# Latent attention: exponentials divided before they are transposed, feature-major output, and output weights split early through DRAM

## The chip, the cores and the metric

The kernel runs on one core of a Trainium2 chip. The metric is device time in microseconds (us), lower is better. The core has five instruction streams: TensorE (PE: matmuls and transposes, with its weight loads, PEld, beside them), VectorE (DVE), ScalarE (ACT), GpSimd (POOL) and SyncE (SP, which here only issues DMA loads). Each stream runs its instructions in order; they wait for one another by semaphores. DMAs are issued by SP, by ACT (stores) or by POOL.

## What is computed

One layer of an encoder for two sequences, a prompt of 256 tokens and a sample of 1024, with the same weights, in fp32. Cut to what the change touches:

```python
h = rmsnorm(x, attn_norm_g); proj = h @ w_in
a = mla_group(...)        # latent attention, 8 heads of 64: softmax(q k^T) v
b = na_group(...)         # neighbourhood attention on a grid, 8 heads of 64
mix = concatenate([rmsnorm(a, mla_out_g), rmsnorm(b, na_out_g)])   # 512 + 512
x = x + mix @ w_o                                                  # 1024 x 1024
h2 = rmsnorm(x, ffn_norm_g)
x = x + (silu(h2 @ w_gate) * (h2 @ w_up)) @ w_down
```

The norm of each half of `mix` is one number per token and half; the gains are folded into the rows of `w_o`.

## The kernel before

The 1280 tokens are ten tiles of 128. To keep fp32 accuracy, operands are split in a high and a low part, and a product is three matmuls, `mm3` (L108 to L112): high by high, high by low, low by high. The stages follow one another on PE, by the time of the profile:

- 0 to 138 us: the first norm, the latents, the rotary keys, the first neighbourhood projections.
- 138 to 193: the values of the neighbourhood attention (L383 to L397). The eight 128x512 blocks of `w_v` are loaded into `wv_raw` slots (eight buffers) and split into `wv_h` on ACT (L134) and `wv_l` on DVE (L135). Then each token tile is 24 matmuls into a PSUM tile `na_t` (two buffers), which ACT copies to `V` (L397).
- 193 to 380: the neighbourhood attention in four pairs of heads. For each pair SP loads tables of bias (`mi_s` and `mp_s` once, then `g_s` and `g_p`), and POOL adds them up to `b_s` (L434) and `b_p` (L449). POOL also splits the weights of the next pair's queries and keys, `wqk_raw` to `wqk_h` and `wqk_l` (L331, L94, L96), and copies queries into zeroed tiles `qz` (L411, L485). The projections of the next pair (`pj`) run on PE between the heads' work.
- 380 to 669: the latent attention, `attend` (L743 to L809). The unit of work is one head `i` of a pair and one chunk of 256 queries, done in two halves `u` of 128. For a half of the sample there are six score matmuls of 128x512 into `S` (128x1024), the negated maximum on DVE (L770), the exponential with its sum `l` on ACT (L772) into `ex` (two buffers), eight PE transposes of 128x128 into `tp` (L778), and their split to `PT`, a copy on ACT (L99) and a subtraction on DVE (L100). After both halves come 16 matmuls `o` (L788), which give a transposed output with the high and the low values' parts in the two halves of its 128 rows. ACT copies it to `os` (L792), PE transposes it back (two of L796), ACT copies it to `ob` (L798), DVE takes reciprocals of the sums (`mr`, L800), POOL adds the two parts (L801) and multiplies by the reciprocal (L805), and ACT's queue stores `at` token-major to `a_d`.
- 660 to 791: output projection, norm and the FFN's input, tile by tile. `mix_in` (L863) loads a token tile's two halves from `a_d` and `b_d`, ACT sums squares (L873), POOL works out the two factors (`rstd_of`) and scales both halves (L877). `mix_T` transposes them (eight `trm`, L888) and splits them to `mT`. `out_proj` (L897) does 24 matmuls for each half of the columns in one PSUM bank `po`, and DVE adds the residual (L907). The output weights are loaded raw before that by SP, and POOL multiplies them by the gain (L855) and splits them (L94, L96), 24 operations in all, between 597 and 639 us.
- 791 to 1610: the FFN.

SP's loads are issued in the order of the program text (`manual_schedule`). The order of the other streams is made by a scheduler from dependences and its own costs. A tile pool of n buffers makes the writer of buffer use k wait for the readers of use k - n, and memory that one pool gives up is handed to later pools, whose first writers then wait for the last users of it.

## Time and profile before

| what | us |
|---|---|
| median of three runs (1612.18 to 1613.88) | 1613.79 |
| span of the profiled execution | 1610.3 |
| PE busy | 1582.5 |
| DVE busy | 893.3 |
| ACT busy | 717.2 |
| POOL busy | 666.1 |

The profiled execution's own time lies within the three runs; its span, from the first instruction to the last, is 3.5 us under the median. In the views a row is a line of the kernel, an engine, an operation and `out<-in`, with a count; then the total busy time and the mean time of one in ns, and the idle time of the engine ahead of it with what ended that. In a timeline row the first number is the start and the second the length. Matmuls overlap: each row's length is longer than the distance to the next. PE's granted clock is 0.99 to 1.00 in all stages.

### The profile page before, as it was taken

Reading aid. Unit: us, or ns where it says so; the run is one execution under the profiler, and the core shown is the slowest. Engines: PE = TensorE matmul, PEld = TensorE weight load, DVE = VectorE, ACT = ScalarE, POOL = GpSimd, SP = SyncE. Lnnn points to the kernel's source line nnn. Section 1 sums busy time; section 2 is a strip of 40 time slices with the busy share of each in tenths; the row PEclk is TensorE's granted clock in tenths of the full one; section 3 lists DMA queues with packets and bytes.
Section 4 is the critical chain, followed back from the end, with each engine's and each line's share of the span. In section 5 each row is a group of like instructions: output and inputs, shape, how many; then the busy total and the mean of one; then the engine's idle time right before and its main releaser. Section 6 shows DMA issues by size and latency. Waiting matters only on the chain.

```text
span 1610.3 us, 25767 instructions
## 1 busy us (share of the span) xinstructions
PE 1582.5 (98%) x9616; PEld 1443.1 (90%) x9616; DVE 893.3 (55%) x1501; ACT 717.2 (45%) x1492; POOL 666.1 (41%) x833
## 2 busy tenths in 40 slices
PE   8999999999999999999999999999999999999998
PEld 8998789998888888888899999999999998888886
DVE  5853045566677777443583444334444246886676
ACT  6533144465777777544453323233222332443334
POOL 4633235544211129224676665565666651010002
PEclk9999999999999999999999999999999999999999
DMA  8626022152100030234312232222232237843534
GB/s 294 202 70 160 19 53 63 37 209 62 32 20 26 24 119 20 80 118 144 125 67 65 89 110 97 71 87 89 97 110 76 70 128 269 296 140 96 157 103 155
DMA packets 121772, 171.09 MB, mean 106 GB/s; under 512 B 35376, under 2 KB 65840, under 8 KB 121648
## 3 DMA queue, kind: packets, MB, share of 16 engines
q1 hardware_dynamic: 78880, 120.30, 24.3%
q10 hardware_dynamic: 41952, 46.08, 8.2%
q0 software_dynamic: 816, 3.08, 0.5%
q8 instruction: 75, 1.23, 0.3%
q14 instruction: 49, 0.40, 0.1%
HBM read 118.96 MB, written 50.46 MB: 105 GB/s over the span
## 4 chain that ended last, share of the span: by engine, by line
PE 90%; POOL 3%; ACT 2%; DVE 2%; DMA 1%; issue 1%; SPq 0%; ACTq 0%; POOLq 0%; DVEq 0%
PE M L112 11%; PE M L110 10%; PE M L111 10%; PE d L111 5%; PE d L110 5%; PE d L112 5%; PE o L788 4%; PE tp L778 4%; PE na_o L512 3%; PE po L110 2%; PE pj L110 2%; PE pj L111 2%; PE pj L112 2%; PE po L111 2%; PE po L112 2%; PE S L110 2%
## 5 line engine op out<-in xcount | busy, mean ns | idle before, releaser
L111 PE MATMUL M<-S,wc 128*128 128x320 f32 x1056 | 323.8, 308 | 0.0
L110 PE MATMUL M<-S,wc 128*128 128x320 f32 x1056 | 321.3, 309 | 2.5 <-ACT S L962 1.2
L112 PE MATMUL M<-S,wc 128*128 128x320 f32 x1056 | 312.0, 309 | 2.4 <-POOL wc L970 2.4
L110 PEld LDWEIGHTS M<-S,wc 128*128 128x128 f32 x1056 | 197.3, 188 | 3.7 <-ACT S L962 1.5
L111 PEld LDWEIGHTS M<-S,wc 128*128 128x128 f32 x1056 | 198.2, 188 | 0.0
L112 PEld LDWEIGHTS M<-S,wc 128*128 128x128 f32 x1056 | 194.7, 188 | 3.0 <-POOL wc L970 3.0
L970 POOL TENSOR_TENSOR wc<-A,wc 128x512 fp32r<-128x512 f32 x86 | 121.1, 1409 | 81.6 <-ACT wc L969 81.5
L1052 DVE TENSOR_TENSOR z<-M,z 128x320 f32<-128x320 f32 x120 | 57.2, 487 | 129.6 <-PE M L112 109.1
L969 ACT CAST wc<-A 128x512 fp32r<-128x512 f32 x86 | 53.5, 622 | 158.4 <-PE M L111 148.8
L970 POOL TENSOR_TENSOR wc<-sum,wc 128x512 fp32r<-128x512 f32 x62 | 88.5, 1427 | 85.8 <-ACT wc L969 85.7
L1052 DVE TENSOR_TENSOR zB<-M,zB 128x320 f32<-128x320 f32 x100 | 47.6, 488 | 133.4 <-PE M L112 109.9
L111 PE MATMUL d<-S,S 128*128 128x512 f32 (+1 forms) x314 | 121.1, 386 | 0.0
L112 PE MATMUL d<-S,S 128*128 128x512 f32 (+1 forms) x314 | 120.7, 386 | 0.0
L110 PE MATMUL d<-S,S 128*128 128x512 f32 (+1 forms) x314 | 120.4, 387 | 0.0
L100 DVE TENSOR_TENSOR PT<-tp,PT 128x512 fp32r<-128x512 f32 (+1 forms) x144 | 93.2, 658 | 33.9 <-ACT PT L99 32.7
L969 ACT CAST wc<-sum 128x512 fp32r<-128x512 f32 x62 | 38.4, 619 | 144.0 <-PE M L111 99.6
L99 ACT CAST PT<-tp 128x512 fp32r<-128x512 f32 (+1 forms) x144 | 79.2, 567 | 33.5 <-PE tp L778 30.2
L770 DVE TENSOR_REDUCE mm<-S 128x1 f32<-128x1024 f32 (+1 forms) x80 | 85.0, 1062 | 13.5 <-PE S L112 11.9
L1099 ACT CAST S<-as 128x640 fp32r<-128x640 f32 x58 | 42.2, 728 | 105.7 <-issue 62.7
L772 ACT ACTIVATE ex<-S,mm 128x1024 f32<-128x1024 f32 (+1 forms) x80 | 79.7, 997 | 14.9 <-DVE mm L770 13.6
L801 POOL TENSOR_TENSOR ob<-ob 128x128 f32<-128x128 f32 x40 | 18.5, 461 | 160.8 <-ACT ob L798 157.3
L788 PE MATMUL o<-PT,v 128*128 128x256 f32 x544 | 80.4, 287 | 0.9 <-ACT PT L99 0.9
(432 smaller groups left out, 4115.8 us busy)
## 6 DMA issues: line engine op xcount, KB each, us to landing
as<-act_d SPq DMA_DIRECT2D x73, 320.0 KB
w<-in_w_down_dram SPq DMA_DIRECT2D x44, 256.0 KB
act_d<-z ACTq DMA_DIRECT2D x35, 320.0 KB
act_d<-zB ACTq DMA_DIRECT2D x35, 320.0 KB
A<-in_w_gate_dram SPq DMA_DIRECT2D x42, 256.0 KB
A<-in_w_up_dram SPq DMA_DIRECT2D x42, 256.0 KB
x<-in_x_tm_dram SPq DMA_DIRECT2D x20, 512.0 KB
cT_d<-stg ACTq DMA_DIRECT2D x20, 320.0 KB
```

Source lines behind the costliest of these rows:

```text
L99: i = nc.scalar.copy(out=hi, in_=ps)
L100: nc.vector.tensor_sub(out=lo, in0=ps, in1=hi)
L110: nc.tensor.matmul(out, lhsT=sh, rhs=mh, start=first, stop=False, **kw)
L111: nc.tensor.matmul(out, lhsT=sh, rhs=ml, start=False, stop=False, **kw)
L112: return nc.tensor.matmul(out, lhsT=sl, rhs=mh, start=False, stop=last, **kw).ins
L770: nc.vector.reduce_max(out=nm[:, u:u + 1], in_=S, axis=AX.X, negate=True)
L772: nc.scalar.activation(ex, S, AF.Exp, bias=nm[:, u:u + 1], scale=1.0, accum_out=l[:, u:u + 1])
L778: nc.tensor.transpose(tp[:, j], ex[:, kt * P:(kt + 1) * P], ident)
L788: nc.tensor.matmul(oT, lhsT=vv, rhs=pt[s][g][:, j], start=kt == 0 and s == 0, stop=kt == nkt - 1 and s == 1)
L969: i0 = nc.scalar.copy(out=hi, in_=raw)
L970: i1 = nc.gpsimd.tensor_tensor(out=lo, in0=raw, in1=hi, op=ALU.subtract)
L1052: nc.vector.tensor_add(out=o, in0=ps, in1=a)
```

## The change

It has three parts.

1. **Attention.** A reciprocal of each half's sums is taken on DVE at once, and POOL multiplies `ex` by it in place, in groups of 512 keys, ahead of the transposes (`ex` gets a third buffer). The output is then divided already. It is not transposed back: ACT copies the two 64-row parts (`os` and `at`, 64x256 each), POOL adds them, and ACT's queue stores `at` feature-major to `aT_d`. The transposes of L796 and the operations of L798, L801 and L805 are gone.
2. **Output weights.** They are loaded, multiplied by the gain and split in the V stage: sixteen blocks of 128x512, each a load of 256 KB on POOL's queue into a `wv_raw` slot, an ACTIVATE on ACT, a `scalar_tensor_tensor` on DVE, and a store of 512 KB on POOL's queue to `wo_d`, through three `wo` buffers. Later eight loads of 1 MB on SP's queue bring them back. The 24 POOL operations are gone. The gain's load moves ahead of the `w_v` loads.
3. **Mixing.** The attention half arrives transposed, so it is split without PE (ACT and DVE). Its squares, summed over features, need a sum across partitions: POOL adds four blocks to one, and a matmul with a column of ones sums that. Neither half is scaled before the projection. `out_proj` accumulates the two halves in two banks, and DVE adds each to the residual with its factor per token (40 `scalar_tensor_tensor` for 20 adds).

```diff
+    for n in range(2 * KC):
+        kc, hs = n // 2, slice(512 * (n % 2), 512 * (n % 2) + 512)
+        raw = rv.tile([P, 512], F32, name="wv_raw", bufs=8)
+        store_p(raw, w_o[kc][:, hs])
+        w = rv.tile([P, 2, 512], F32R, name="wo", bufs=3)
+        nc.scalar.activation(w[:, 0], raw, AF.Copy, scale=gm[:, kc:kc + 1])
+        nc.vector.scalar_tensor_tensor(out=w[:, 1], in0=raw, scalar=gm[:, kc:kc + 1],
+                                       in1=w[:, 0], op0=ALU.mult, op1=ALU.subtract)
+        store_p(wo_d[kc, :, :, hs].bitcast(F32), w.bitcast(F32))
...
-                    ex = p2.tile([P, 1024], F32, name="ex", bufs=2)[:, 0:ntok]
+                    ex = p2.tile([P, 1024], F32, name="ex", bufs=3)[:, 0:ntok]
...
+                    r = p2.tile([P, 1], F32, name="mr", bufs=4)
+                    nc.vector.reciprocal(r, l[:, u:u + 1])
                     for g in range(ngrp):
+                        es_ = ex[:, g * gk * P:(g + 1) * gk * P]
+                        nc.gpsimd.tensor_scalar(out=es_, in0=es_, scalar1=r, scalar2=1.0,
+                                                op0=ALU.mult, op1=ALU.mult)
...
-                os_ = p2.tile([P, 256], F32, name="os", bufs=2)
-                nc.scalar.copy(out=os_, in_=oT)
-                op = pp.tile([P, 512], F32, name="o", bufs=2)[:, 0:256]
-                for u in range(2):
-                    us = slice(u * P, (u + 1) * P)
-                    last_os[0] = nc.tensor.transpose(op[:, us], os_[:, us], ident).ins
...
+                own, oth = slice(DH * i, DH * i + DH), slice(DH - DH * i, 2 * DH - DH * i)
+                nc.scalar.copy(out=os_[own], in_=oT[oth])
+                nc.scalar.copy(out=at[own], in_=oT[own])
+                nc.gpsimd.tensor_tensor(out=at[own], in0=at[own], in1=os_[own], op=ALU.add)
             row = base + c * 256
-            store(a_d[row:row + 256, p * P:(p + 1) * P].rearrange("(u t) f -> t u f", u=2), at)
+            store(aT_d[p, :, row:row + 256], at)
...
+    def load_wo(kc):
+        wt = rw.tile([P, 2, D], F32R, name=f"wo{kc}")
+        load_r(wt, wo_d[kc])
+        wo.append(wt)
...
-        load(mx[:, 0:512], a_d[ts_, :])
+        at = mx[:, 0:512].rearrange("p (c q) -> p c q", c=4)
+        load(at, aT_d[:, :, ts_].rearrange("c p t -> p c t"))
         load(mx[:, 512:], b_d[ts_, :])
-        mn = rm.tile([P, D], F32, name="m", bufs=3)
+        mT = (rt1 if t % 2 else rt0).tile([P, 2, KC, P], F32R, name=f"mT{t % 2}")
+        nc.scalar.copy(out=mT[:, 0, 0:4], in_=at)
+        nc.vector.tensor_sub(out=mT[:, 1, 0:4], in0=at, in1=mT[:, 0, 0:4])
+        sq = rm.tile([P, D], F32, name="m", bufs=3)
         ss = rm.tile([P, 2], F32, name="ssm", bufs=2)
+        nc.scalar.activation(sq[:, 0:512], mx[:, 0:512], AF.Square)
+        for n in (2 * P, P):
+            mixed[0] = nc.gpsimd.tensor_tensor(out=sq[:, 0:n], in0=sq[:, 0:n],
+                                               in1=sq[:, n:2 * n], op=ALU.add).ins
+        tr = po.tile([P, 4, P], F32, name="trm", bufs=1)
+        for kc in range(4):
+            nc.tensor.transpose(tr[:, kc], mx[:, 512 + kc * P:512 + (kc + 1) * P], ident)
+        last_split[0] = split_ps(mT[:, 0, 4:8], mT[:, 1, 4:8], tr)
+        nc.scalar.activation(sq[:, 512:], mx[:, 512:], AF.Square, accum_out=ss[:, 1:2])
+        ps = pm[0].tile([P, 512], F32, name="M0", bufs=4)[:, 0:1]
+        nc.tensor.matmul(ps, lhsT=sq[:, 0:P], rhs=ones[:, 0:1], start=True, stop=True)
+        nc.vector.tensor_copy(out=ss[:, 0:1], in_=ps)
...
+            for n, ps in enumerate((pm[0].tile([P, 512], F32, name="M0", bufs=4),
+                                    po.tile([P, 512], F32, name="po", bufs=2))):
...
+                    for kc in range(4 * n, 4 * n + 4):
+                        last = mm3(ps, mT[:, 0, kc], mT[:, 1, kc], wo[kc][:, 0, hs],
+                                   wo[kc][:, 1, hs], kc == 4 * n, kc == 4 * n + 3)
+                nc.vector.scalar_tensor_tensor(out=x[:, hs], in0=ps, scalar=r[:, n:n + 1],
+                                               in1=x[:, hs], op0=ALU.mult, op1=ALU.add)
```

How the change moves instructions, in rows of the streams' order (line, operation, `out<-in`, shape, count of like rows in a run; the changed kernel's lines are about a dozen higher from the V stage on).

POOL before, from the last rotary factors `rc` to the first bias sums:

```order
L222 TENSOR_TENSOR rc<-rc,mhalf 128x2
L411 MEMSET qz_2074 64x128
L411 MEMSET qz_2075 64x128
L411 MEMSET qz_2076 64x128
L411 MEMSET qz_2077 64x128
L485 COPY qz_2074<-qa 64x128
L485 COPY qz_2076<-qb 64x128
L485 COPY qz_2075<-qa 64x128
L485 COPY qz_2077<-qb 64x128
L434 TENSOR_TENSOR b_s<-g_s,mi_s 128x128 x12
L449 TENSOR_TENSOR b_p<-g_p,mp_s 128x128 x8
L331 TENSOR_TENSOR wqk_raw<-wqk_raw,ga 128x512 x2
```

POOL now, at the same place: the start of the 32 output-weight DMAs (a raw load is `wv_raw<-in_w_o_dram`, a store `wo_d<-wo`), which go on alternating store and load,

```order
L219 TENSOR_SCALAR rc<-ssc 128x1
L221 TENSOR_SCALAR rc<-ssc 128x1
L223 TENSOR_TENSOR rc<-rc,mhalf 128x2
L71 DMA wv_raw<-in_w_o_dram 128x512 x8
L71 DMA wo_d<-wo 256x1x512
L71 DMA wv_raw<-in_w_o_dram 128x512
```

and their end:

```order
L71 DMA wv_raw<-in_w_o_dram 128x512
L71 DMA wo_d<-wo 256x1x512 x8
L423 MEMSET qz_2173 64x128
L423 MEMSET qz_2174 64x128
L423 MEMSET qz_2175 64x128
L423 MEMSET qz_2176 64x128
L497 COPY qz_2173<-qa 64x128
```

All 32 stand ahead of the `qz` tiles, the bias sums and the pair's weights. On SP's queue the `mi_s` load, and with it all later loads, now waits for DVE's split of the sixteenth block (`mi_s` takes over memory of the V stage's tiles).

ACT before, in the V stage:

```order
L364 CAST kb<-pj 64x512
L365 CAST kb<-pj 64x512
L397 COPY V<-na_t 128x512 x10
L500 ACTIVATE na_sb,na_l<-na_sb,na_m 128x256
L507 COPY na_pt<-na_t 128x256
```

ACT now, at the same place, where the block's ACTIVATE waits for a `wo` buffer, that is for the store three blocks back:

```order
L365 CAST kb<-pj 64x512
L366 CAST kb<-pj 64x512
L399 ACTIVATE wo<-wv_raw,gm 128x512 x2
L409 COPY V<-na_t 128x512 x2
L399 ACTIVATE wo<-wv_raw,gm 128x512 x2
L409 COPY V<-na_t 128x512
L399 ACTIVATE wo<-wv_raw,gm 128x512 x3
L409 COPY V<-na_t 128x512
```

The V copies stand between and behind the weights' ACTIVATEs.

PE before, in the latent attention of the last pair of heads, between the scores of two halves of queries:

```order
L112 MATMUL S_7664<-mk1o,mq1A 128x512
L796 MATMUL o<-ident,os 128x128 x2
L778 MATMUL tp<-ident,ex 128x128 x8
L110 MATMUL S_7688<-mk1o,mq1A 128x512
L111 MATMUL S_7688<-mk1o,mq1A 128x512
L112 MATMUL S_7688<-mk1o,mq1A 128x512
```

PE now, between the scores of the same two halves:

```order
L113 MATMUL S_7765<-mk1o,mq1A 128x512
L805 MATMUL o<-PT,v_4850 128x256
L805 MATMUL o<-PT,v_4860 128x256
L795 MATMUL tp<-ident,ex 128x128 x4
L805 MATMUL o<-PT,v_4850 128x256
L805 MATMUL o<-PT,v_4860 128x256
L111 MATMUL S_7793<-mk1o,mq1A 128x512
```

The two transposes of `os` are gone, and the transposes of `ex` come in other groups, each behind a scaling on POOL.

More of the change, by code (lines that the diff above doesn't have):

```diff
@@ L47, in encoder_trunk @@
     kr_d = tc.dram_tile([2, RD, NTOK], F32R, name="kr_d")
[L48 removed]
+    aT_d = tc.dram_tile([PAIRS, P, NTOK], F32, name="aT_d")
+    wo_d = tc.dram_tile([KC, P, 2, D], F32R, name="wo_d")
     b_d = tc.dram_tile([NTOK, 512], F32, name="b_d")
@@ L382, in encoder_trunk @@
     rv = pool("rv", side="right")
+    gm = rv.tile([P, KC], F32, name="gm")
+    load(gm, g_mix)
     wv = []
@@ L874, in mix_in @@
         rstd_of(r, ss, 512)
[L875 to L890 removed]
+        return mT, r
@@ L1000, in encoder_trunk @@
     pm = [pool("pm0", space=PSUM)]
-    for n, (pl, nm) in enumerate(((rw, "wo4"), (rw, "wo5"), (rw, "wo6"), (rt0, "mT0"))):
-        load_wo(n, pl, nm)
-    cur = mix_T(0, mix_in(0))
+    for kc in range(KC):
+        load_wo(kc)
+    cur = mix_in(0)
     load(gf, g_ffn)
```

66 lines of the change are left out of this document (11 added, 55 removed).

## Prediction

> **What bounds the kernel now.** I read the page first, then the busy time by stage, then the groups of instructions, and last the timelines of the two stretches that the change touches. The page's first part and its row of gigabytes per second (40 slices of 40.3 us):
>
> ```profile
> PE 1582.5 (98%) x9616; PEld 1443.1 (90%) x9616; DVE 893.3 (55%) x1501; ACT 717.2 (45%) x1492; POOL 666.1 (41%) x833
> GB/s 294 202 70 160 19 53 63 37 209 62 32 20 26 24 119 20 80 118 144 125 67 65 89 110 97 71 87 89 97 110 76 70 128 269 296 140 96 157 103 155
> ```
>
> TensorE (PE) is busy for 1582.5 of 1610.3 us. The busy time of each engine in the stages that the change touches (PE, weight loads, DVE, ACT, POOL, then granted clock and DMA share) says whether that holds in each of them:
>
> ```profile
> 137.70:193.20 55.50, 55.28 (x240) 44.73 (x239) 6.48 (x10) 11.41 (x20) 19.75 (x32) 1.00 0.24 54
> 380.00:669.00 289.00, 284.54 (x1845) 250.16 (x1846) 207.87 (x317) 208.17 (x442) 89.60 (x139) 1.00 0.13 41
> 669.00:791.00 122.00, 121.93 (x598) 98.92 (x597) 43.83 (x65) 46.96 (x115) 45.95 (x67) 1.00 0.38 127
> ```
>
> It does: PE is idle for 0.2 us in the V stage, 4.5 us in the latent attention and 0.1 us in the output projection. So a PE instruction that goes is worth its pace, as long as no other engine is late, and work put on DVE, ACT, POOL or DMA is free as long as it is on time for PE. The median of the runs, 1613.79 us, is 3.5 us above the span of the profiled execution; I sum against the span and add the difference to that median.
>
> **Transposes that go.** The chain of waits gives pieces of pure pace, and the groups give what goes:
>
> ```profile
> 390.27 0.87 PE tp L778 x8
> 407.55 1.87 PE o L788 x16
> 223.12 1.28 PE na_o L512 x12
> L796 PE MATMUL o<-ident,os 128*128 128x128 f32 x80 | 15.5, 275 | 0.1
> L888 PE MATMUL trm<-ident,m 128*128 128x128 f32 x80 | 12.1, 273 | 0.0
> ```
>
> Matmuls overlap, so the 275 ns of one is not what it costs; eight transposes of the same 128x128 fp32 kind take 0.87 us, 0.109 each. The 80 of L796 go: 80 x 0.109 = 8.7 us. Half of the 80 of L888 go: 40 x 0.109 = 4.4 us. Ten new matmuls with the ones column come. The trace has none of one column; the nearest row is the fp32 one with 64 columns (na_o, 1.28/12 = 0.107 us), and most of the ten stand beside fp32 transposes, so no change of kind is added. I take 10 x 0.11 = +1.1; the bounds are 0 and 0.35 each (3.5 in all, if each also waits a quarter microsecond for the sum of squares). The split of the projection's accumulation into two banks leaves its 480 matmuls as they are. PE thus loses 8.7 + 4.4 - 1.1 = 12.0 us of work.
>
> **Can the others keep up in the latent attention?** The groups of one head's work there:
>
> ```profile
> L770 DVE TENSOR_REDUCE mm<-S 128x1 f32<-128x1024 f32 x64 | 78.2, 1222 | 7.7 <-PE S L112 6.1
> L100 DVE TENSOR_TENSOR PT<-tp,PT 128x512 fp32r<-128x512 f32 x128 | 86.5, 687 | 30.2 <-ACT PT L99 29.2
> L772 ACT ACTIVATE ex<-S,mm 128x1024 f32<-128x1024 f32 x64 | 72.0, 1126 | 14.6 <-DVE mm L770 13.3 <-POOL at L805 1.3
> L99 ACT CAST PT<-tp 128x512 fp32r<-128x512 f32 x128 | 73.1, 591 | 32.1 <-PE tp L778 29.1 <-PE o L788 0.6
> L792 ACT COPY os<-o 128x256 f32<-128x256 f32 x40 | 14.9, 373 | 13.3 <-PE o L788 13.0
> L800 DVE RECIPROCAL mr<-ml 128x2 f32<-128x2 f32 x40 | 6.3, 159 | 8.6 <-ACT ex L772 8.1
> L877 POOL TENSOR_SCALAR m<-m,rm 128x512 f32<-128x512 f32 x20 | 13.6, 693 | 1.0
> L801 POOL TENSOR_TENSOR ob<-ob 128x128 f32<-128x128 f32 x40 | 18.5, 461 | 160.8 <-ACT ob L798 157.3 <-DVE mr L800 3.4
> ```
>
> One head and one 256-query chunk is a unit. Two units lie between two like places of PE's timeline, the rows at 641.14 and 654.44 below, so one takes 13.30/2 = 6.65 us:
>
> ```profile
> 641.14 1.04 PE L778 MATMUL tp<-ident,ex 128*128 128x128 f32 x8
> 642.25 0.40 PE L111 MATMUL S<-mk0o,mq0B 128*128 128x512 f32 x1
> 643.18 0.40 PE L112 MATMUL S<-mk0o,mq0B 128*128 128x512 f32 x1
> 651.47 0.60 PE L778 MATMUL tp<-ident,ex 128*128 128x128 f32 x4
> 654.44 1.04 PE L778 MATMUL tp<-ident,ex 128*128 128x128 f32 x8
> ```
>
> The rows at 642.25 and 643.18 are four score matmuls apart: 0.93/4 = 0.23 each. After the change a unit needs of PE 12 score matmuls (2.8), 16 transposes (16 x 0.109 = 1.7) and 16 output matmuls (16 x 1.87/16 = 1.9): 6.4 us. DVE needs two maxima, four subtractions and now two reciprocals: 2.44 + 2.75 + 0.32 = 5.5. ACT needs two exponentials (each with a read of the accumulator, some 0.2), four casts, and two copies that have half the partitions and the same 256 columns, which I keep at 0.373: 2.65 + 2.36 + 0.75 = 5.8. POOL needs four scalings of 128x512, which are those of L877 in kind and shape (0.693), and an add of 256 columns, at most twice the 128-column 0.461: 2.8 + 0.9 = 3.7. All stay below PE's 6.4. ACT comes nearest, with 0.6 us a unit to spare.
>
> The new wait is in depth: exponential, reciprocal, scaling, then transposes. What covers it now:
>
> ```profile
> 647.28 1.14 ACT L772 ACTIVATE ex<-S,mm 128x1024 f32<-128x1024 f32 x1
> ```
>
> That exponential ends at 648.4 and its transposes come at 651.47: 3.1 us of cover. The reciprocal and the first scaling take 0.16 + 0.69, with hops about 1.0, and the second half's scaling follows 0.7 later, so some 2 us of cover is left. The third `ex` buffer lets the exponential run further ahead. In-order POOL has this scaling behind only short adds. I charge 0.7 us for waits at the places where the head order changes, between -2 (part of the 4.5 us idle goes with the os chain) and +3. If the cover were gone, PE would wait at its transposes unit by unit, and what it saves there would be lost again: rival 2.
>
> **In the output projection** DVE gets 20 more operations on a bank. The old L907 add took 0.69, so +13.8 us beside 43.8 of 122 busy; POOL trades 20 scalings for 20 adds; a tile's statistics now end after its transposes, but r is needed only at the banks' end, half a tile of PE work later. All hidden: 0 (0 to 2, inside the 3 above).
>
> **The split of the output weights in the V stage.** This is the uncertain term. Rows of the split in use today, of what follows it on SP's queue and on POOL, and of PE's first uses:
>
> ```profile
> L134 ACT ACTIVATE wv_h<-wv_raw,ga x8: 707/712/725, 136.5 to 142.1; 128x512 fp32r<-128x512 f32 x8
> L135 DVE SCALAR_TENSOR_TENSOR wv_l<-wv_raw,ga,wv_h x8: 743/746/752, 137.3 to 142.9; 128x512 fp32r<-128x512 f32 x8
> 136.56 0.33 SPq L64 DMA_DIRECT2D mi_s<-in_m_int_dram  x1
> 137.96 8.15 SPq L64 DMA_DIRECT2D g_s<-in_rpb_s_dram  x16
> 148.44 5.02 POOL L434 TENSOR_TENSOR b_s<-g_s,mi_s 128x128 f32<-128x128 f32 x12 [17.98 <-DMA g_p<-in_rpb_p_dram]
> 153.42 3.38 POOL L449 TENSOR_TENSOR b_p<-g_p,mp_s 128x128 f32<-128x128 f32 x8
> 159.93 2.54 POOL L96 TENSOR_TENSOR wqk_l<-wqk_raw,wqk_h 128x512 fp32r<-128x512 f32 x2
> 200.93 0.28 PE L112 MATMUL pj<-hT_h,wqk_l 128*128 128x256 f32 x1
> ```
>
> In the changed order SP's `mi_s` load waits for DVE's sixteenth output-weight split, and POOL's bias sums stand behind the sixteenth store. Call the end of that split T. Before, `mi_s` was issued at 136.56 and the first half of pair 1's low weights was ready at 159.93 + 1.27 = 161.2, that is 24.6 later (with a hop, 24.9). PE uses it at 200.93. So PE stalls by S = max(0, T - 176.0). Queued behind the waiting SP load are all bias and pair weight loads; behind POOL's stores the `qz` copies and bias sums; behind ACT's waiting ACTIVATEs the V copies, which PE's V tiles need. Those copies are less tight: the last follow T, and PE has two V tiles (11.1 us of the 193.2) left then, so they bite from T = 181.8, in the same stall.
>
> T itself: there are three `wo` buffers, so weight k waits for store k-3. The first store is issued after eight raw loads, the last of which waits for the end of the wv split, 142.9 + 0.75 = 143.65; with its issue, 144.4. Then come the stores of weights 0, 3, 6, 9 and 12 in a chain, each followed by one ACT and one DVE operation (0.71 + 0.75 = 1.46): T = 144.4 + 5 x (L + 1.46) = 151.7 + 5L, where L is from the start of a store's issue to its landing. The rows for L, transfers of the same software queue:
>
> ```profile
> b_d<-b_s POOLq DMA_DIRECT2D x1, 512.0 KB, 3.9
> act_d<-z POOLq DMA_DIRECT2D x7, 320.0 KB, 7.9
> L70 POOL DMA_DIRECT2D b_d<-b_s x2: 735/854/974, 376.1 to 381.1; - x2
> DMA to landing us min/median/max: 3.9/4.5/6.1
> q1 hardware_dynamic: 78880, 120.30, 24.3%
> ```
>
> The first is the same size, alone on its queue: 3.9 gives T = 171.2 and no stall, and with the 0.85 of its issue outside the 3.9, 175.4 and none either. The second, seven stores close together, gives T = 191.2 and S = 15.2. The Trainium skill (DMA: Bandwidth & Descriptors, Anatomy of one DMA — SWDGE (gpsimd) path) puts a transfer of this path at 2.0 us plus its bytes by 436e3 per us. That is 3.2 us for 512 KB as an estimate, T = 167.7 and no stall; both rows of this trace are longer. Here up to three stores share the engines with the raw loads, as neither row has it. The traffic is 16 x (256 + 512) KB = 12.6 MB; q1 moved 120.30 MB in 24.3% of 1610.3 us, 307 GB/s while busy, and the fullest slice of the page is 296. At 307 the traffic takes 41 us from the first raw load at 138.1, so until 179.1. I take T = 179, L = 5.5, between the 512 KB row with its issue (4.75) and the longest of the 3.9/4.5/6.1 row: S = +3.0 us, with 0 to 15.2 as ends. Later, POOL is rid of the old split and SP gets eight loads of 1 MB long before 659; 0.
>
> **The sum.** -12.0 + 0.7 + 3.0 = -8.3: a span of 1602.0 and a time of 1613.79 - 8.3 = 1605.5 us.
>
> **Rivals.**
> 1. The weights' trip is fully hidden (L up to 4.86). For it: the 3.9 row, and DMA at 24% of that stage. Against it: the demand is above any rate that the page shows. -11.3, 1602.5 us. The skill's fit for that path, cited above, would have this outcome. Chance 0.27.
> 2. The latent attention gives nothing back: PE saves 8.7 there and waits as much for scaled exponentials or ACT's copies (0.6 us a unit in hand; some 2 of depth). Against it: today's idle of 4.5 us in 289 and the longer lead by a third buffer. -12.0 + 8.7 + 3.0 = -0.3, 1613.5 us: no change. Chance 0.14.
> 3. Slower: the stores land as `act_d` does. The place is the first pair of the neighbourhood attention, where PE waits at 200.93 for weights (and at its V tiles before), at 5 us for each microsecond of L beyond 4.86. It eats the 11.3 at S = 11.3, L = 7.1; at 7.9 it is -11.3 + 15.2 = +3.9, 1617.7 us. For it: the only row with several stores in flight; against it: those wait on other traffic of their stage too, and the 512 KB row is half as long. Chance 0.13, of which 0.10 past the point at which it is slower by over 0.2%.
> 4. The change undoes itself at the junction: the projection's first tile waits for its feature-major half or the 1 MB weight loads. The old chain (load, squares, scaling, transposes, split) was longer than the new one. Some 3 us at most, in the range. Chance 0.08.
>
> **How the numbers follow.** The forecast (S between 0.5 and 7, 1603 to 1610) has 0.38. A measurement of this kernel tells about 0.2%, 3.2 us, from no change: faster is below 1610.6, slower above 1617.0. Faster: nearly all of 0.38, all of 0.27, some of rivals 2 and 4: 0.70. Same: most of rival 2 and the middle of rivals 3 and 4: 0.18. Slower: 0.12. The range runs from -12.0 - 2 = -14, 1599.8, to 1615.0, which takes in rival 2 and leaves out the far part of rival 3.
>
> **What would show it.** Right: no L796 and 40 trm transposes, a unit of 6.4 us in PE's timeline between 520 and 650, PE idle of 5 to 6 us in that stage, the sixteenth weight ACTIVATE near 178, and one wait of PE of about 3 us around 193 to 215. Wrong: units still of 6.65 with `tp` waiting for POOL (rival 2); the sixteenth ACTIVATE after 185 with PE idle over 9 us between 176 and 215 (rival 3), or before 176 with none (rival 1).

## The result and the profile after

The changed kernel takes 1626.14 us (median of four runs, 1624.4 to 1629.43) against 1612.99 for the kernel before beside it (1611.95 to 1613.88). The ratio is 1.0082, with a 95% interval of 1.007 to 1.0094: slower by 13 us, where 8.3 us faster was forecast. The span went from 1610.3 to 1623.3 us. PE's busy time is lower than before and the kernel is longer all the same. Two executions far out of line (1770 us in run 8, 6239 us of the kernel before beside runs 16 to 18) are left out of every median and ratio below. The first part of the page after:

```profile
PE 1577.7 (97%) x9516; PEld 1437.9 (89%) x9516; DVE 932.1 (57%) x1587; ACT 731.2 (45%) x1498; POOL 742.6 (46%) x945
```

I split the program at four points of PE's timeline: the first V matmul (137.50 before, 137.76 after), the first latent score (380.32 and 385.18), the last row of output matmuls `o` (664.18 and 677.88) and the first FFN matmul (791.21 and 804.71). Between the first two the time rose by 4.6 us, from the first score to the FFN by 8.6, and the FFN fell by 0.5. The busy time by stage, before and then after (latent attention, then output projection; behind the length come PE, weight loads, DVE, ACT and POOL, then the granted clock, the DMA share and GB/s):

```profile
380.32:664.18 283.86, 279.40 (x1813) 245.62 (x1812) 207.76 (x316) 207.68 (x441) 89.60 (x139) 1.00 0.14 42
664.18:791.21 127.03, 126.96 (x627) 103.32 (x626) 44.03 (x65) 47.55 (x117) 45.95 (x67) 1.00 0.36 122
```

```profile
385.18:677.88 292.70, 273.24 (x1730) 237.64 (x1730) 210.04 (x355) 209.96 (x439) 142.24 (x216) 1.00 0.16 55
677.88:804.71 126.83, 124.73 (x609) 102.66 (x609) 66.18 (x97) 47.31 (x110) 51.62 (x71) 1.00 0.36 122
```

In the latent attention PE is busy for 6.2 us less and stands idle for 19.5 us instead of 4.5. What it waits for there, by PE's waits of that stage (engine, operand, line; what it waits for; total, times, longest):

```profile
PE tp L795 <- DVE PT L101: 12.6, 16, 1.4
PE S L111 <- ACT ex L784: 2.7, 6, 0.5
PE o L805 <- ACT PT L100: 2.4, 5, 0.7
```

PE does not wait for the scaled exponential, the wait that I had looked for. Its transposes wait for a free `tp` bank: there are two, and a bank is free when ACT has cast it and DVE has subtracted it (L100, L101). One such place in the timeline after:

```profile
534.32 1.04 PE L795 MATMUL tp<-ident,ex 128*128 128x128 f32 x8
534.51 0.36 ACT L812 COPY os<-o 64x256 f32<-64x256 f32 x1 [1.28 <-PE o L805]
534.90 0.37 ACT L813 COPY at<-o 64x256 f32<-64x256 f32 x1
535.29 0.59 ACT L100 CAST PT<-tp 128x512 fp32r<-128x512 f32 x1
535.91 0.69 DVE L101 TENSOR_TENSOR PT<-tp,PT 128x512 fp32r<-128x512 f32 x1 [0.65 <-ACT PT L100]
536.75 0.63 PE L795 MATMUL tp<-ident,ex 128*128 128x128 f32 x4 [1.40 <-DVE PT L101]
```

PE has a row of twelve transposes: eight fill both banks, and the last four need the first bank again. Its cast stands on ACT behind both output copies, its subtraction ends at 536.60, and PE has waited 1.40 us. In the changed order there are 8 such rows of twelve, in the order before none; 9.1 of the 12.6 us stand at the ninth transpose of these eight rows. In a steady pair of heads (from the first prompt score of a pair to that of the next) this takes 70.9 us, against 68.85 before.

In the V stage the `mi_s` load, which waits for DVE's sixteenth split, went out at 178.46; the split thus ended near the 179 forecast. The stores, and what ACT waited for at its weight operations:

```profile
178.46 0.33 SPq L65 DMA_DIRECT2D mi_s<-in_m_int_dram  x1
DMA to landing us min/median/max: 3.1/4.3/6.8
L399 ACT ACTIVATE wo<-wv_raw,gm 128x512 fp32r<-128x512 f32 x16 | 11.4, 722 | 11.7 <-DMA wo_d<-wo 9.4 <-DVE wo L400 1.3 <-issue 1.0
```

PE waits 0.86 us at 204.21 for POOL's low weights of the next pair. The rest of the loss shows in the granted clock, the column ahead of the DMA share, at the start of the neighbourhood attention, after:

```profile
193.00:197.00 4.00, 2.66 (x14) 1.63 (x12) 0.96 (x5) 1.63 (x5) 4.00 (x11) 1.00 0.56 149
197.00:201.00 4.00, 4.00 (x19) 3.70 (x20) 1.92 (x9) 2.32 (x7) 4.00 (x9) 0.57 0.00 0
201.00:205.00 4.00, 3.14 (x19) 2.49 (x19) 0.78 (x2) 0.00 (x0) 4.00 (x5) 0.91 0.12 33
205.00:209.00 4.00, 4.00 (x18) 3.60 (x18) 0.00 (x0) 0.00 (x0) 0.38 (x1) 0.66 0.57 156
```

It drops twice, each time behind a stretch in which PE was busy for only 2.7 to 3.1 of 4 us, and PE then does less in the same time.

### The profile page after: what moved, and what is told of

It reads as the page before. It is cut to its first block, busy times and chain, and to the rows that moved or that the text cites. A ratio compares the mean times of both kernels' runs of the same rounds, so it can differ in the third digit from the quotient of the medians.

```text
span 1623.3 us, 26060 instructions
## 1 busy us (share of the span) xinstructions
PE 1577.7 (97%) x9516; PEld 1437.9 (89%) x9516; DVE 932.1 (57%) x1587; ACT 731.2 (45%) x1498; POOL 742.6 (46%) x945
## 4 chain that ended last, share of the span: by engine, by line
PE 51%; POOL 1%; DVE 1%; ACT 0%; issue 0%; DMA 0%; SPq 0%; POOLq 0%; DVEq 0%; ACTq 0%
PE M L111 11%; PE M L113 11%; PE M L112 11%; PE d L112 5%; PE d L111 5%; PE d L113 5%; POOL wc L969 0%; PE po L112 0%; PE po L111 0%; PE po L113 0%; PE trh L925 0%; DVE m L916 0%; DMA A<-in_w_down_dram 0%; POOL A L947 0%; POOL rh L92 0%
## 5 line engine op out<-in xcount | busy, mean ns | idle before, releaser
L790 POOL TENSOR_SCALAR ex<-ex,mr 128x512 f32<-128x512 f32 (+1 forms) x144 | 95.7, 677 | 105.7 <-DVE mr L787 73.9
L101 DVE TENSOR_TENSOR PT<-tp,PT 128x512 fp32r<-128x512 f32 (+1 forms) x144 | 92.4, 657 | 41.3 <-ACT PT L100 40.6
L100 ACT CAST PT<-tp 128x512 fp32r<-128x512 f32 (+1 forms) x144 | 78.6, 562 | 37.3 <-PE tp L795 36.3
L795 PE MATMUL tp<-ident,ex 128*128 128x128 f32 x544 | 79.4, 273 | 12.7 <-DVE PT L101 12.6
```

Source lines behind the costliest of these rows:

```text
L100: i = nc.scalar.copy(out=hi, in_=ps)
L101: nc.vector.tensor_sub(out=lo, in0=ps, in1=hi)
L790: nc.gpsimd.tensor_scalar(out=es_, in0=es_, scalar1=r, scalar2=1.0, op0=ALU.mult, op1=ALU.mult)
L795: nc.tensor.transpose(tp[:, j], ex[:, kt * P:(kt + 1) * P], ident)
```

## The experiments

There were 18 runs, numbered in their order. Three lengths tell the stages apart: **V** from the first V matmul to the first latent score, **pair** the third period from a pair's first prompt score to the next pair's, **LM** from the first latent score to the first FFN matmul. The ratio stands against the kernel before on the same chip. Runs 3, 6, 10, 12, 14 and 18 leave the division of the attention's output out, and run 8 takes the output weights of rows 512 to 1023 for rows 0 to 511 too: these runs are for timing alone.

| run | us | ratio, 95% interval | V | pair | LM |
|---|---|---|---|---|---|
| before | 1612.99 | | 242.8 | 68.85 | 410.9 |
| after | 1626.14 | 1.0082 (1.0070 to 1.0094) | 247.4 | 70.9 | 419.5 |
| 1 weights late | 1634.78 | 1.0136 (1.0121 to 1.0151) | 242.7 | 70.6 | 434.3 |
| 2 weights early alone | 1620.59 | 1.0044 (1.0029 to 1.0058) | 246.8 | 68.9 | 414.2 |
| 3 no scaling | 1632.48 | 1.0118 (1.0103 to 1.0133) | 246.3 | 73.2 | 427.2 |
| 4 three `tp` banks | 1621.75 | 1.0055 (1.0038 to 1.0072) | 244.0 | 67.9 | 417.0 |
| 5 PE's old order | 1662.88 | 1.0304 (1.0286 to 1.0323) | 246.1 | 81.8 | 458.1 |
| 6 = 5, no scaling | 1647.60 | 1.0216 (1.0199 to 1.0233) | 246.6 | 75.9 | 439.0 |
| 7 = 5, weights late | 1670.20 | 1.0354 (1.0339 to 1.0370) | 242.7 | 84.8 | 468.0 |
| 8 = 5, half the early traffic | 1659.67 | 1.0291 (1.0274 to 1.0309) | 243.5 | 81.6 | 456.1 |
| 9 reciprocal on POOL | 1628.29 | 1.0093 (1.0078 to 1.0108) | 246.7 | 71.7 | 423.0 |
| 10 = 5, no division | 1647.12 | 1.0203 (1.0182 to 1.0223) | 247.3 | 75.9 | 440.8 |
| 11 = 5, reciprocal on POOL | 1667.62 | 1.0339 (1.0323 to 1.0354) | 246.1 | 80.4 | 461.5 |
| 12 no division | 1630.34 | 1.0110 (1.0092 to 1.0128) | 247.0 | 73.1 | 425.8 |
| 13 = 5, two `ex` buffers | 1640.80 | 1.0169 (1.0154 to 1.0185) | 247.2 | 77.2 | 435.1 |
| 14 = 10, two `ex` buffers | 1622.25 | 1.0052 (1.0035 to 1.0068) | 245.8 | 70.0 | 417.6 |
| 15 two `ex` buffers | 1639.49 | 1.0160 (1.0145 to 1.0175) | 246.3 | 74.5 | 431.5 |
| 16 = 4, single `o` bank relieved | 1615.64 | 1.0016 (1.0005 to 1.0028) | 244.4 | 68.2 | 412.0 |
| 17 = 16, one ACT copy, 12 early blocks | 1614.56 | 1.0011 (0.9996 to 1.0025) | 243.4 | 67.4 | 411.0 |
| 18 = 14, one ACT copy | 1618.42 | 1.0033 (1.0020 to 1.0045) | 248.5 | 69.7 | 414.8 |

### The output weights: runs 1, 2, 7, 8

Run 1 undoes part 2 of the change: the raw loads, multiplications and splits go back to their late place on POOL.

```diff
-    for n in range(2 * KC):
-        kc, hs = n // 2, slice(512 * (n % 2), 512 * (n % 2) + 512)
...
-    for kc in range(KC):
-        load_wo(kc)
+    for n, (pl, nm) in enumerate(((rw, "wo4"), (rw, "wo5"), (rw, "wo6"), (rt0, "mT0"))):
+        load_wo(n, pl, nm)
```

> The changed kernel with the output weights loaded and split late on POOL, as before the change; attention and mixing stay changed. Theory A (the early split stalls the first pair of the neighbourhood attention by the 4.9 us by which the first scores of the latent attention come later, and the latent attention loses the rest by itself): about 1621, with the first latent scores near 380.3. Rival B (the early split costs nothing, the whole loss lies in the latent attention and the mixing): 1626, with the first scores still near 385.

V is back at 242.7, as theory A said, but LM rises by 14.8, which neither theory expected, and both expected times are missed. PE's waits in the latent attention now have a line for POOL, whose late splits stand ahead of the scalings:

```profile
PE tp L784 <- DVE PT L101: 11.8, 15, 1.4
PE tp L784 <- POOL ex L779: 5.7, 3, 3.8
```

These 5.7 us are not all of the 14.8: the scores' waits for the exponentials rise from 2.7 to 6.7 us, and the granted clock, 1.00 there in the changed kernel, is 0.57 from 620 to 628 and 0.60 from 644 to 648. So with the new attention the early split is the better place, by 8.6 us in all; yet it is not free. Run 2 puts only part 2 (the same lines with + and -) into the kernel before.

> The kernel before with only the early split of the output weights (V stage, through DRAM); attention and mixing as before. Theory A: 1613.0 + 4.9 = about 1618, all of it lost between 193 and 260 us. Rival B: 1613, within 2 us.

V rises by 4.0, near the 4.6 of the changed kernel, and LM, which theory A left alone, by 3.3: the pairs keep 68.9, but the last pair's order is a new one, with waits for `tp` banks of 0.64 and 0.78 where the old one had none. The rest of the 3.3 is not traced. Runs 7 and 8 are on the base of run 5 below; 7 has run 1's edit, 8 splits only the last eight blocks early.

```diff
-    for n in range(2 * KC):
+    for n in range(KC, 2 * KC):
...
-        load_r(wt, wo_d[kc])
+        load_r(wt, wo_d[4 + kc % 4])
```

> The pinned order and the output weights split late on POOL as before the change. Theory A: the first latent scores come 4.9 us earlier than with the early split, but POOL's 24 operations of 1.1 to 2.4 us (28 us in all) stand ahead of scalings in POOL's queue near 600-640 us and PE waits there for some 5-9 us: 1612-1618. If the scalings were free of them: 1607.

> The pinned order, and only half of the output weights split early: the eight blocks of rows 512 to 1023, which are then loaded for rows 0 to 511 too, so half of the projection uses wrong weights and the V stage has half the traffic. Theory A (the early split stalls the neighbourhood attention because the bias loads wait for its last block, at 177.7 us): the last split ends near 158-162, the stall goes, the first latent scores are at 380-381, and the total is 4-5 us under the pinned kernel. Rival: the loss before the latent attention is of another kind (the clock, the loads through DRAM as such) and stays.

V is 242.7 without early weights and 243.5 with half of them (`mi_s` out at 158.94). The 4.6 us of the V stage thus come with the weights' trip. Run 7's time is far from the 1612 to 1618 expected, as this base was slow in the attention (run 5); run 8 is 3.2 us under run 5, where 4 to 5 were expected.

### What is new in the attention, at the scheduler's order: runs 3, 9, 12, 15

```diff
-                        nc.gpsimd.tensor_scalar(out=es_, in0=es_, scalar1=r, scalar2=1.0,
-                                                op0=ALU.mult, op1=ALU.mult)
```

> The changed kernel without POOL's multiplication of the exponentials, so the attention's output is not divided by the sums. Theory A (PE waits in the latent attention because three groups of transposes come in a row and there are two tp banks; five such rows of twelve are left here, of eight): the idle time of that stage falls from 19.2 to 10-13 us, about 1618-1621. Rival C (PE waits for the scaled exponentials): the idle time falls to the 4.7 of before, about 1611.

Without the scaling it got slower, by 7.6 us of LM, where both theories expected it faster. The wait for the banks stayed, though this order has five rows of twelve in place of eight:

```profile
PE tp L792 <- DVE PT L101: 12.4, 19, 1.2
```

Run 9 takes the 80 reciprocals from DVE to POOL (a power of -1), run 12 leaves out reciprocals and scalings, run 15 gives `ex` its two buffers back.

```diff
-                    nc.vector.reciprocal(r, l[:, u:u + 1])
+                    nc.gpsimd.tensor_tensor(out=r, in0=l[:, u:u + 1], in1=mhalf[:, 2:3], op=ALU.pow)
```

> The changed kernel with the 80 reciprocals (128x1) taken off DVE's queue: POOL raises the sum to the power -1 and then scales as before. The pinned runs fell far behind even without the scaling (1648 us), so the order of TensorE alone is not the cause. Theory D: the reciprocal stands in DVE's in-order queue right behind each maximum, waits there for ACT's exponential (15.1 us of DVE's idle time in the changed kernel, 34.6 to 39.5 in the pinned ones), and the subtractions behind it free the tp banks late. Then without it the idle time of the latent attention falls from 19.5 to 5-10 us: 1611-1617. Rival A (bunched transposes): this order has four rows of twelve, of eight, so about half of the loss: 1617-1621. Rival E (whatever the cause, ACT's order of exponentials and casts sets it): 1622-1630.

> The changed kernel without reciprocals and without scaling (no division), with the scheduler's own order, which has four rows of twelve transposes. Against the run without scaling but with reciprocals (1632.5 us): theory D expects 1611-1616; rival A about 1616-1622; rival E 1625-1635.

```diff
-                    ex = p2.tile([P, 1024], F32, name="ex", bufs=3)[:, 0:ntok]
+                    ex = p2.tile([P, 1024], F32, name="ex", bufs=2)[:, 0:ntok]
```

> The changed kernel with two ex buffers and the scheduler's own order (nine rows of twelve transposes). Theory F alone: faster than the changed kernel, 1612-1620. If the uneven order on TensorE and DVE costs by itself (rows of twelve with two tp banks): 1624-1632.

All three are slower than the changed kernel, by 3.5, 6.3 and 12.0 us of LM; theory D and theory F fell at this order. The number of rows of twelve, four, four and nine against eight in the changed kernel, does not order the times either. Neither reciprocals, scalings nor the third buffer is by itself what makes the changed kernel slow. But each edit also moves the scheduler's order on all engines, and so these runs can't price the edit at a given order.

### PE's old order by hand: runs 5, 6, 10, 11, 13, 14, 18

Run 5 keeps the changed kernel's instructions and chains PE's, from the latent attention to the FFN, in the order of the kernel before, less what is gone (a table `ORDER`). DVE, ACT and POOL stay with the scheduler.

```diff
+    for m, n in zip(seq, seq[1:]):
+        tc.add_manual_dep(pe[n], pe[m].name, mybir.DependencyInfo(
+            mybir.DependencyClass.NoSync, mybir.DependencyReason.DATA), reason="order")
```

> The changed kernel with TensorE's order in the latent attention pinned to that of the kernel before, without the 80 removed transposes (1760 instructions; nothing else changed, the other engines' order is again the scheduler's). Theory A (the loss in the latent attention is the new order: transposes in rows of twelve with two tp banks): idle time of that stage from 19.5 to 5-8 us, from the first latent scores to the first FFN matmul 403-408 us instead of 419.5 (410.9 before), total about 1611-1615, with the V stage's 5 us still lost. Rival C (PE waits for the scaling on POOL): the transposes wait for POOL at the old places instead, the stage stays near 419, total 1622-1628.

The theory that PE's new order alone is the fault fell: 81.8 us a pair, longer than either theory allowed. The next four take away, at this order, the scaling (6), the whole division (10), DVE's reciprocals (11, run 9's edit) and the third `ex` buffer (13).

> As the kernel with the pinned order, but without POOL's multiplication of the exponentials (the attention's output is not divided by the sums). Theory A: the scaling is hidden at that order, so within 2 us of the pinned kernel. Rival C: 6 us or more faster than the pinned kernel.

> TensorE's order pinned to that of the kernel before, and neither reciprocals nor scaling (the attention's output is not divided by the sums). Theory D: the idle time of the latent attention is back at 5-10 us of the kernel before, from the first latent scores to the first FFN matmul 401-408 us, 1608-1615 in all. Rival E: it stays near the 1648 of the pinned kernel without scaling but with reciprocals.

> TensorE's order pinned to that of the kernel before, the reciprocal on POOL, with the scaling. Theory D: 1612-1620 (the scaling is hidden but for some waits at those places). Rival C (the scaling on POOL is late at that order): 10 us or more above the pinned kernel without scaling and reciprocals. Rival E: 1650-1663.

> The changed kernel with two ex buffers, as before, and TensorE's order pinned to that of the kernel before. Its order on ACT repeats exponential, cast, the two output copies, cast, exponential, cast, cast, and on DVE maximum, reciprocal, subtraction, subtraction, as the kernel before does; with three buffers the casts and subtractions come in uneven groups. Theory F (the third buffer: what ACT and DVE do first): from the first latent scores to the first FFN matmul 403-412 us instead of 458, 1611-1620 in all. Rival G (the feature-major output, or the wait for the scaled exponentials): it stays over 1640.

> The same without reciprocals and scaling (the attention's output is not divided by the sums). Theory F: 401-406 us for that stretch, 1609-1614 in all; the difference to the run with them is the price of the divide. Rival G (feature-major output): over 1640. If only the divide is late: 1609-1614 here, over 1640 there.

The waits of the latent attention in run 5, then in runs 13 and 14, and last the busy time of runs 13 and 14 there:

```profile
PE tp L828 <- DVE PT L133: 25.2, 18, 2.4
PE tp L828 <- POOL ex L823: 15.1, 11, 1.8
```

```profile
PE tp L828 <- POOL ex L823: 15.0, 11, 1.8
PE tp L828 <- DVE PT L133: 3.0, 9, 1.3
```

```profile
PE tp L823 <- DVE PT L133: 6.8, 8, 2.2
PE o L833 <- DVE PT L133: 2.1, 3, 0.8
```

```profile
385.06:695.26 310.20, 284.40 (x1746) 243.03 (x1745) 210.27 (x356) 211.21 (x439) 141.52 (x216) 0.98 0.15 52
383.88:676.24 292.36, 277.50 (x1746) 239.21 (x1745) 199.94 (x276) 209.68 (x439) 47.05 (x72) 1.00 0.16 55
```

The 25.2 us of run 5 all stand at the fifth transpose of a row of eight, of which the kernel before has 30 without such a wait. So rows longer than the ring are not needed for it: it also depends on when ACT and DVE free a bank.

Run 6 is 15.3 us faster than run 5, so at this order the scaling is not hidden, as rival C had it. Runs 6 and 10 are alike (439.0 and 440.8): the reciprocals cost nothing, and moving them (11) gains nothing. Runs 13 and 14 differ by the division: 17.5 us of LM. The transposes wait 15.0 us for POOL in run 13; as other waits are shorter there, PE is idle for 25.8 us against 14.9. The other 6.9 us are busy time, at a granted clock of 0.98 against 1.00 (0.79 from 576 to 592). So at PE's old order rival 2's wait is real; in the changed kernel, with its other groups, it does not occur. Two buffers in place of three take 23 us at this order in both pairs of runs (5 to 13, 10 to 14) and cost 12 at the scheduler's (15). Theory D fell here too, and runs 13 and 14 missed the times of theory F. Even run 14, without any division, needs 70.0 a pair, where 68.85 less 20 transposes of 0.109, the 80 of four pairs, would be 66.7. Run 18 tries whether the two ACT copies of the output are the reason:

```diff
-                nc.scalar.copy(out=at[own], in_=oT[own])
-                nc.gpsimd.tensor_tensor(out=at[own], in0=at[own], in1=os_[own], op=ALU.add)
+                nc.vector.tensor_add(out=at[own], in0=oT[own], in1=os_[own])
```

> The kernel with PE's old order written out by hand, two ex buffers and no division at all (its output leaves out the softmax division), in which a pair takes 69.9 us where 66.9 would be the old 68.85 less the 20 transposes; and in it the second ACT copy and the POOL add are replaced by one DVE add. PE's order is the same. If the two ACT copies in one go, between two casts, are what keeps the pair from its 66.9: 67 to 68.5 us a pair and 1612 to 1617 us. If the copies don't matter: 69.5 to 70.2 a pair, 1621 to 1623.

69.7 against 70.0 a pair: at this order the copies are not what keeps the pair from 66.7. They are not free either: LM falls by 2.8 and the time by 3.8 us, to 1618.42, between the two ranges expected. Its V of 248.5 is that of the profiled execution, the longest of nine, in which the clock dropped early.

### Banks and copies: runs 4, 16, 17

Run 4 gives the transposes a third bank and takes it from `o`.

```diff
-                        tp = pp.tile([P, 4, P], F32, name="tp", bufs=2)[:, 0:gk]
+                        tp = pp.tile([P, 4, P], F32, name="tp", bufs=3)[:, 0:gk]
...
-                oT = pp.tile([P, 512], F32, name="o", bufs=2)[:, 0:256]
+                oT = pp.tile([P, 512], F32, name="o", bufs=1)[:, 0:256]
```

> The changed kernel with three tp banks and one o bank in place of two and two. Theory A: the waits of the transposes for DVE's split go, the idle time of the latent attention falls from 19.2 to 5-9 us, about 1612-1616. Rival C: the wait is for the exponentials, 1626 within 2 us. Should the single o bank cost, it shows as waits of o or of the projections for ACT.

```profile
PE o L111 <- DVE v L101: 5.0, 4, 1.6
PE tp L795 <- DVE PT L101: 0.7, 1, 0.7
```

The wait of 12.6 us is down to 0.7 and the pair to 67.9, but the time, 1621.75, misses theory A's 1612 to 1616. PE now waits for the one `o` bank, which also serves the value products. Run 16 gives those (and the small score banks) a `tp` bank:

```diff
-            pv = pp.tile([P, 512], F32, name="o", bufs=2)
+            pv = pp.tile([P, 4, P], F32, name="tp", bufs=3).rearrange("p a b -> p (a b)")
...
-        return pp.tile([P, 512], F32, name="o", bufs=2)
+        return pp.tile([P, 4, P], F32, name="tp", bufs=3).rearrange("p a b -> p (a b)")
```

> The changed kernel with three tp banks and one o bank, as in the run with three tp banks, but the value products of make_V and the small score banks, which take an o bank there, take a tp bank instead, so that the single o bank serves the latent output alone. If the two tp banks under rows of twelve transposes are what makes the pair slow, and the slow first pair of 82.2 us in that run came only from make_V's single bank: all four pairs at 67.9 to 69.5 us (70.6 to 70.9 in the changed kernel, 68.8 before), the latent stage with mixing about 408 to 412 us (419.5; before 410.9), time 1609 to 1616. If a third tp bank only moves the wait to the single o bank, the pairs stay at 70 or more and the time at 1620 or more.

The first pair keeps its 81.2 us, against the expectation. Most of that is a mark in another place: pair 1's first prompt score stands 13.8 us behind the first latent score there, in the changed kernel 20.5, and 481 matmuls lie up to the next pair's mark, in the changed kernel 427. From the first latent score to the second pair's mark it is 95.0 us, against 91.1 in the changed kernel and 92.2 before. The other pairs take 68.2, LM 412.0 and the time 1615.64, as expected if the banks are the cause; this order still has eight rows of twelve. Stage and waits in run 16:

```profile
381.51:666.86 285.35, 270.17 (x1730) 238.25 (x1730) 208.63 (x356) 209.27 (x439) 141.62 (x216) 0.99 0.17 58
```

```profile
PE S L111 <- ACT ex L784: 7.8, 8, 1.3
PE S L111 <- POOL mk0o L633: 2.6, 1, 2.6
PE o L805 <- ACT PT L100: 2.0, 3, 0.7
PE tp L795 <- DVE PT L101: 0.7, 1, 0.7
```

PE's busy time is now down by 9.2 us against before, and 10.7 us of new idle time eat it. The next wait in line is that of the scores for the exponential that frees their banks, for which this timeline of run 16 shows the reason:

```profile
497.20 1.20 DVE L782 TENSOR_REDUCE mm<-S 128x1 f32<-128x1024 f32 x1
498.13 0.37 ACT L813 COPY at<-o 64x256 f32<-64x256 f32 x1
498.52 0.59 ACT L100 CAST PT<-tp 128x512 fp32r<-128x512 f32 x1
499.01 1.12 ACT L784 ACTIVATE ex<-S,mm 128x1024 f32<-128x1024 f32 x1
500.27 0.50 PE L111 MATMUL S<-mk1o,mq1C 128*128 128x512 f32 x1 [1.26 <-ACT ex L784]
```

The maximum is there at 498.40; ACT is in the second output copy and then in a cast, and the exponential starts 0.6 us later. Run 17 takes that copy away (run 18's edit) and, in the other stage, splits only twelve blocks early, the last four late on POOL (`range(12)` for `range(2 * KC)`).

> As the run before it in this list (three tp banks, one o bank for the latent output alone), and two things more: DVE adds the bank's half to os straight into at, which replaces the second ACT copy and the POOL add; and only the twelve blocks of the weights' rows 0 to 767 are split early, the last four blocks late on POOL as before. The two act in different stages. Second ACT copy: if two copies in one go between two casts cost the pair, its periods fall by another 0.5 to 1.5 us against the run before it; if not, they stay within 0.3. Fewer early blocks: DVE's last early split comes near 168 instead of 178, so that PE's wait and the clock's drop in the neighbourhood stage go (first latent score 242.7 to 243.5 us after the first V matmul, 247.4 in the changed kernel), against up to 4 us for eight late POOL operations ahead of scalings at 617 to 645. Time 1604 to 1612 if all holds; by the rivals 1612 to 1620.

```profile
PE S L111 <- ACT ex L784: 5.5, 8, 1.2
PE tp L795 <- POOL ex L790: 2.8, 3, 1.4
PE S L111 <- POOL mk0o L633: 2.6, 1, 2.6
```

The pair is 67.4 and V 243.4, both as expected; the time, 1614.56 us, is in the rivals' range and not measurably different from before. The two middle pairs, which had 137.7 us before, have 134.6, but the first, up to the second's mark, gives 3.6 back and the last 0.5. The first has the wait of 2.6 for `mk0o`, POOL's memsets, in runs 16 and 17 alike. No version beat the kernel before.

## Why the prediction was wrong, point by point

**The sum.** Forecast -8.3, measured +13.0 of span, 21.3 apart: 1.6 in the V stage, 19.9 from the first score to the FFN, and -0.2 elsewhere. The 19.9 are 14.3 of idle in the latent attention (15.0 more, 0.7 charged), 2.0 of idle in the projection, and 3.6 of PE's busy time that did not go (6.2 and 2.2 in place of 8.7 and 3.3).

**The step that failed** is "The new wait is in depth", with its 0.7 us for waits "at the places where the head order changes". I compared the other engines' work per unit with PE's 6.4 us and looked for the one added wait, that for the scaling. The durations were right; these are the groups after:

```profile
L790 POOL TENSOR_SCALAR ex<-ex,mr 128x512 f32<-128x512 f32 x128 | 88.0, 702 | 91.2 <-DVE mr L787 61.8 <-PE tp L795 14.3 <-PE S L113 9.6
L812 ACT COPY os<-o 64x256 f32<-64x256 f32 x40 | 14.7, 367 | 20.0 <-PE o L805 19.5
L787 DVE RECIPROCAL mr<-ml 128x1 f32<-128x1 f32 x80 | 12.6, 158 | 15.4 <-ACT ex L784 15.1
```

702, 367 and 158 ns against the 693, 373 and 159 I took. But PE's two `tp` banks go round PE, ACT and DVE in order, and at the new order, above all in its eight rows of twelve transposes, PE needs a bank again before ACT and DVE have freed it: 12.6 us in all. That ring was in no term of the sum. Run 16 shows its price: with a third bank 11.9 us of that wait and 7.5 us of LM go, with eight rows of twelve still in the order, and PE's busy time falls by what was forecast (9.2 against 8.7). Why ACT and DVE free the banks late in some orders, as in run 5 at rows of eight, and in time in the kernel before, is not settled.

**Transposes that go** were removed, as forecast, but not their time: run 17, with a third bank and one copy less, comes to 67.4 a pair, near the 66.7 of the forecast's pace, and even there the first and last pair hand the gain back. Each of these edits also moved the scheduler's order on the other engines, so the split between banks and copies (run 17 says 0.8 us a pair for a copy, run 18 says 0.3) stays open, as does what holds run 14's order at 70.0.

**Rival 2** had the right outcome, that the attention gives nothing back, for the wrong wait; in length the attention went 8.8 us past that (283.86 to 292.70). The changed kernel has no wait for POOL's scalings; it shows at other orders, with 15.0 us in run 13, 5.7 in run 1 and 2.8 in run 17.

**The V stage.** T was right (179, `mi_s` at 178.46), in part by luck. One store of the chain, and the ACTIVATE that waited for it:

```profile
171.66 0.68 POOL L71 DMA_DIRECT2D wo_d<-wo  x1 [0.55 <-DVE wo L400]
176.92 0.72 ACT L399 ACTIVATE wo<-wv_raw,gm 128x512 fp32r<-128x512 f32 x1 [1.96 <-DMA wo_d<-wo]
```

That is 5.3 us; the five of the chain took 6.0, 4.3, 5.6, 3.7 and 5.3, on average 5.0 in place of L = 5.5. But from such an ACTIVATE to the next store's issue there were 1.80 us in place of 1.46, and the first store went out at 144.88 in place of 144.4, so the errors nearly cancel. The landings that the views give are counted from the issue, so the 3.9 has the issue in it, and 4.75 counts it twice; the 6.1 of the third row is a store of 64 KB. The direct stall is smaller than the 3.0 charged: runs 4 and 16, with the same early weights and full clock, have V at +1.2 and +1.6. The rest of +4.6 is the clock, which the sum left out. Rivals 1 and 3 did not come, though the chain's 5.0 is near the 4.86 of rival 1.

**The output projection** was put at 0 and has 2.0 us of idle: PE's FFN-input transposes wait for DVE, 0.17 to 0.81 each at five places. DVE has 20 more operations on a bank there, of 0.75 us; that these make it late is argued, not tried:

```profile
L905 DVE SCALAR_TENSOR_TENSOR x<-M,rm,x 128x512 f32<-128x512 f32 x20 | 15.0, 751 | 26.9 <-PE M L113 24.2 <-POOL rm L92 1.4 <-POOL zA L947 1.3
```

"Half a tile of PE work later" covered the factors but not what follows the banks on DVE. Rival 4's junction held.

## What to carry to other kernels

An engine that is busy 98% of the time says how little idle time there is, not that work taken from it comes back as time: the removed work may have been the time in which another engine freed its buffers. Before costing a removal at full pace, follow each ring of two buffers that the engine writes into: look in the new order for runs of writes longer than the ring, and ask when the engines that free a buffer get to it. Where a scheduler makes the order, an edit can't be priced by taking it out alone; fix the order of one engine too, and read the waits, not only the time.

## What the runs showed of the hardware

The granted clock fell behind short waits of PE. In the changed kernel, where none of them is over 0.9 us, it is 0.50 from 198 to 200:

```profile
198.00:200.00 2.00, 2.00 (x11) 1.96 (x10) 0.75 (x4) 1.32 (x5) 2.00 (x6) 0.50 0.00 0
```

Run 4, with the same weights and like gaps, has 1.00 in the same windows:

```profile
193.00:197.00 4.00, 2.99 (x18) 2.15 (x17) 1.85 (x8) 2.65 (x8) 4.00 (x11) 1.00 0.26 105
197.00:201.00 4.00, 3.96 (x28) 3.12 (x26) 1.92 (x7) 1.07 (x3) 4.00 (x7) 1.00 0.06 16
```

Of the profiled executions of the 15 kernels with all sixteen blocks early, 13 show such a drop between 193 and 220 us, with V at +3.0 to +5.7; of the five without it or with fewer blocks, none does. PE's waits from 50 to 85 us behind the first V matmul, those over 0.15 us added up, come to 1.9 to 3.9 us in the 13, to 1.8 and 2.3 in runs 4 and 16, and to 1.0 to 1.5 in the five. That the waits bring the drop is thus likely, but not shown. The Trainium skill (TensorE: Matmul & The Clock Gate, A second HAM failure mode: psum-queue depth-cycling) says that frequent micro-idles between groups of matmuls can make the clock go back and forth between half and full; the 0.50 agrees. Why runs 4 and 16 were spared is not settled. A drop can also stand in the latent attention, as in run 16 behind the wait of 2.6 us for `mk0o` at 387.16, where two 4-us windows show it:

```profile
384.00:388.00 4.00, 1.40 (x6) 0.84 (x5) 1.80 (x3) 2.15 (x4) 3.87 (x9) 0.95 0.69 202
388.00:392.00 4.00, 4.00 (x14) 3.16 (x14) 1.62 (x3) 1.18 (x4) 4.00 (x9) 0.62 0.00 0
```
